# A fused LoRA kernel: how the first load of x is cut over partitions

## The chip, the cores and the metric

The kernel runs on one core of one Trainium2 chip. The metric is device time in microseconds for one execution; lower is better. The kernel before took 123.53 us (median of three runs, 123.52 to 123.67).

A core has TensorE (PE, matrix products), VectorE (DVE), ScalarE (ACT), GpSimd (POOL) and SyncE (SP), which here issues all transfers. Transfers between the chip's main memory and the on-chip memory (128 partitions, each a row of bytes) are carried out by 16 DMA engines. A transfer increments a semaphore by 16 when it is complete, and other engines wait for that count.

## The reference

```python
x: (16, 512, 768) float32    A: (768, 16)    B: (16, 768)    scale = 0.5

lora = np.matmul(np.matmul(x, A), B)
return (x + scale * lora).astype(np.float32)
```

x is 8192 tokens of 768 numbers, 25.2 MB; the result is as large. Every byte of x is read once and every byte of the result is written once.

## The kernel before

A tile is 128 tokens, one in each partition, 768 numbers (3 KB) each. The 64 tiles are cut into five parts of 8, 8, 16, 16 and 16 tiles (`PARTS`). Within a part, each partition holds consecutive tokens: a part of 8 tiles gives a partition one run of 8 x 3 KB = 24 KB of main memory, and a transfer of n tiles of it takes n x 3 KB from each partition's run. x stays in one buffer, `x_sb`, which has room for the first four parts; the fifth reuses the first's and second's room. The sum is written over x there and stored from there.

Loads are listed by part, first tile and number of tiles:

```python
LOADS = [
    (0, 0, 2), (0, 2, 6), (1, 0, 8), (2, 0, 8), (2, 8, 8), (3, 0, 16), (4, 0, 8), (4, 8, 8)
]
```

Load 0 brings two tiles (128 rows of 6 KB), load 1 the other six of part 0 (128 rows of 18 KB). Load k has a semaphore `s_load[k]` of its own.

SP issues in this order (`on_sync`, line 136): load 0, load 1 (line 139), after a wait the rows of A in three transfers (line 156; 12 rows of 4 KB to partitions 0 to 11), after another wait the rows of B (line 160; 16 rows of 3 KB to every fourth partition from 0), then loads 2 to 5. When the sums of the first two parts are done, and PE has reached a certain place in the third group, it issues stores 0 and 1 (line 149); when store 0 has landed, load 6 goes into its room, and load 7 when store 1 has. Stores 2 and 3 follow their sums, and store 4 is issued at the end (line 356).

Compute goes by groups of 8 tiles. `narrowed` (line 188) casts half a group from float32 to float16 (line 196): it waits for the loads that hold the tiles (line 193), once per engine and load. In the first group POOL casts tiles 0 and 1 (load 0), and ACT casts tiles 2 and 3 and then 4 to 7 (load 1). In later groups ACT casts the first four tiles and POOL the other four. DVE turns the result in blocks (line 255), PE multiplies with a spread-out A (line 285, `ps_yt`), ACT scales into `y_bd` (line 240), PE multiplies with B (line 306, `lora_ps`), and DVE adds that to x (line 260).

The weights are prepared at the beginning: DVE turns A's rows (line 248), after A's transfers and POOL's first cast; POOL then casts B (line 214), and makes `w_one` and `w_bd` (lines 216 and 222) from the turned A. PE needs `w_bd` and the turned x before its first product of line 285.

Every engine runs its own written order; semaphores connect them.

Of the kernel before, what the change touches and what calls it, by code (L numbers as in the profile page):

```python
# [28 lines left out]
def kernel(  # L29
# [10 lines left out]
    P = 128  # L40
# [3 lines left out]
    x2 = x.flatten_outer_dims()  # L44
# [38 lines left out]
    def sem(name):  # L83
        sems.append(nc.alloc_semaphore(name))
        return sems[-1]
# [10 lines left out]
    def memory(t2, i, s, n):  # L96
        S = PARTS[i]
        return t2[ds(parts[i], S * P), :].rearrange("(p s) d -> p s d", s=S)[:, ds(s, n), :]

    def held(i, s, n):  # L100
        return tiles(where.index((i, s)), n)

    def tiles(t, n):
        return x_all[:, ds(t % ROOM, n), :]

    LOADS = [
        (0, 0, 2), (0, 2, 6), (1, 0, 8), (2, 0, 8), (2, 8, 8), (3, 0, 16), (4, 0, 8), (4, 8, 8)
    ]
    s_load = [sem(f"s_load{k}") for k in range(len(LOADS))]

    def load_of(t):
        i, s = where[t]
        return next(k for k, ld in enumerate(LOADS) if ld[0] == i and ld[1] <= s < ld[1] + ld[2])
# [21 lines left out]

    def on_sync(e):
        def load(k):
            ld = LOADS[k]
            e.dma_start(out=held(*ld), in_=memory(x2, *ld)).then_inc(s_load[k], 16)  # L139

        def summed(k):
            e.wait_ge(s_sum, k + 1)
            if STORED[k] + 1 < NG:

                e.sem_inc(s_free[PAIRS - 1], 1)

        def store(k, done):
            st = STORES[k]
            e.dma_start(out=memory(out2, *st), in_=held(*st)).then_inc(done, 16)

        load(0)
        load(1)
        e.wait_ge(s_ready, 1)
        blocks = A.rearrange("(c e) r -> c (e r)", e=64)
        for c in range(SETS):
            e.dma_start(
                out=a_rows[c : SET * SET : SET, :], in_=blocks[ds(c * SET, SET), :]
            ).then_inc(s_a, 16)
        e.wait_ge(s_brows, 1)
        e.dma_start(out=b_rows[0 : R * APART : APART, :], in_=B).then_inc(s_b, 16)  # L160
        for k in range(2, len(LOADS) - 2):
            load(k)

        for p in range(2, PAIRS):
            e.sem_inc(s_free[p], 1)
        summed(0)
        summed(1)


        e.wait_ge(s_lora, 2 * PAIRS + 2)  # L170
        store(0, s_out0)
        store(1, s_out1)
        e.wait_ge(s_out0, 16)
        load(len(LOADS) - 2)
        e.wait_ge(s_out1, 16)
        load(len(LOADS) - 1)
        for k in range(2, len(STORES)):
            summed(k)
            if k == 2:


                e.wait_ge(s_raise, 6)
            if k + 1 < len(STORES):
                store(k, s_out)
# [3 lines left out]
    def narrowed(e, copy, g, first, n=SUB):  # L188
        t = g * GROUP + first
        for k in dict.fromkeys(load_of(t + k) for k in range(n)):  # L190
            if (e, k) not in here:
                here.add((e, k))
                e.wait_ge(s_load[k], 16)
        if g:
            e.wait_ge(s_taken, g)
        ins = copy(out=xn[:, ds(first, n), :], in_=tiles(t, n))  # L196

        ins.then_inc(s_narrow if g else s_first if first else s_a, 1)

    def on_gpsimd(e):  # L200
        e.memset(a_rows[0:Q], 0.0).then_inc(s_ready, 1)  # L201
        e.memset(b_rows, 0.0).then_inc(s_brows, 1)  # L202
        e.memset(pick, 0.0).then_inc(s_pick, 1)
        e.memset(w_bd.rearrange("p c k m -> p (c k m)").bitcast(fp32), 0.0)  # L204
        e.memset(y_bd.rearrange("p s m -> p (s m)").bitcast(fp32), 0.0).then_inc(s_ready, 1)  # L205
        e.wait_ge(s_pick, 1)
        e.affine_select(  # L207
            out=pick, in_=pick, compare_op=mybir.AluOpType.not_equal, fill=1.0, base=0,
            pattern=[[0, NQ], [-APART, Q]], channel_multiplier=1,
        ).then_inc(s_pick, 1)  # L210
        narrowed(e, e.tensor_copy, 0, 0, SUB // 2)
        e.wait_ge(s_pick, 2)
        e.wait_ge(s_b, 16)
        e.tensor_copy(out=b_half, in_=b_rows).then_inc(s_bh, 1)  # L214
        e.wait_ge(s_ready, 3)
        e.tensor_copy(  # L216
            out=w_one.rearrange("i (c e) k r -> i c e (k r)", c=SETS),
            in_=a_t[0:Q].rearrange("i k r (e c) -> i c e (k r)", c=SET)[:, 0:SETS, 0:SET, :],
        ).then_inc(s_w, 1)
        e.wait_ge(s_w, 1)  # L220
        for b in range(NQ):
            e.tensor_copy(  # L222
                out=w_bd[ds(b * Q, Q), :, :, ds(b * Q, R)], in_=w_one
            ).then_inc(s_w, 1)
            e.wait_ge(s_w, b + 2)
        for g in range(1, NG):
            narrowed(e, e.tensor_copy, g, SUB)

    def on_scalar(e):
        narrowed(e, e.copy, 0, SUB // 2, SUB // 2)  # L230
        narrowed(e, e.copy, 0, SUB)
        e.wait_ge(s_bp, 1)
        e.copy(out=b_mm, in_=lora[0][:, 0, :]).then_inc(s_bm, 1)  # L233
        for g in range(NG):
            if g + 1 < NG:
                narrowed(e, e.copy, g + 1, 0)
            e.wait_ge(s_y, g + 1)
            for b in range(NQ):
                q = ds(b * Q, Q)
                last = e.mul(out=y_bd[q, :, q], in_=y_ps[q, :, :], mul=sc)  # L240
                if b == 0 and g + 1 < NG:

                    last.then_inc(s_narrow, 1)
            last.then_inc(s_spread, 1)
# [151 lines left out]
```

## Time and profile before

| What | Value |
|---|---|
| median of three runs | 123.53 us |
| the profiled execution's own time | 123.47 us |
| its span | 121.7 us |
| DMA packets (rows and small completion writes) | 1928, 50.43 MB |
| DMA engines' packet time, share of 16 engines' span | 97.0% |
| DVE busy | 81.7 us (67%) |
| PE busy | 50.7 us (42%) |
| ACT busy | 37.4 us (31%) |
| POOL busy | 28.4 us (23%) |

The span is from the first to the last instruction on the core; the time has a small part around it. The page divides the span into 40 slices of 3.04 us: a digit is the busy share in tenths, and a row in GB/s says what the DMA engines moved. A table of stretches gives the same for stretches that one chooses. In a row of the timeline, the bracket says how long the engine had been idle and what released it.

### The profile page before, as it was taken

The page shows a single profiled execution, that of the slowest core. Times are in us where ns is not written, and L with a number is a line of the kernel's source. Part 1 is how long each engine was busy: PE and PEld are TensorE (multiplying, and loading weights), DVE is VectorE, ACT ScalarE, POOL GpSimd, SP SyncE. Part 2 cuts the span into 40 slices and gives each one's busy share as a digit, 9 for nine tenths or more (in the row PEclk, how much of TensorE's full clock was granted, in tenths as well). Part 3 has the DMA queues.
Part 4 walks back from the last instruction along what each step waited for, and adds up shares of the span by engine and source line. Part 5 has one row for each costly group of instructions (what it writes and reads, how often), then busy time and mean ns, then how long its engine had stood idle before and what let it go on. Part 6 is the DMA issues. An engine that isn't in the chain of part 4 may idle for free.

```text
span 121.7 us, 889 instructions
## 1 busy us (share of the span) xinstructions
PE 50.7 (42%) x322; PEld 29.6 (24%) x322; DVE 81.7 (67%) x42; ACT 37.4 (31%) x43; POOL 28.4 (23%) x24
## 2 busy tenths in 40 slices
PE   0000239477457647745745744774674320000000
PEld 0000026243323424423423322442442110000000
DVE  0002850599999999999999989999995991000000
ACT  4003928526409313644440192733004000000000
POOL 7721638017009002604400170710000000000000
PEclk9999999999999999999999999999999995555555
DMA  3999999999998997999999999997998899799790
GB/s 65 442 418 440 444 420 428 444 420 428 477 517 355 420 517 307 452 412 436 452 396 428 460 404 436 469 517 323 452 517 388 388 517 436 339 517 452 323 517 0
DMA packets 1928, 50.43 MB, mean 414 GB/s; under 512 B 236, under 2 KB 236, under 8 KB 392
## 3 DMA queue, kind: packets, MB, share of 16 engines
q1 hardware_dynamic: 1928, 50.43, 97.0%
HBM read 25.26 MB, written 25.17 MB: 414 GB/s over the span
## 4 chain that ended last, share of the span: by engine, by line
DVE 34%; DMA 28%; PE 10%; ACT 9%; issue 1%; SPq 0%; POOLq 0%
DVE x_sb L260 22%; DMA x_sb<-in_x_dram 20%; DVE xt L255 12%; DMA out_dram<-x_sb 8%; PE ps_yt L285 6%; ACT xn L196 6%; PE lora_ps L306 3%; ACT y_bd L240 3%; SPq L139 0%; SPq L391 0%; POOLq L134 0%; POOLq L377 0%
## 5 line engine op out<-in xcount | busy, mean ns | idle before, releaser
L260 DVE TENSOR_TENSOR x_sb<-x_sb,lora_ps 128x1536 f32<-128x1536 f32 x32 | 53.7, 1734 | 1.4 <-PE lora_ps L306 1.4
L306 PE MATMUL lora_ps<-b_mm,y_bd 128*128 128x512 f16 (+1 forms) x128 | 25.0, 328 | 22.4 <-ACT y_bd L240 14.1
L196 ACT CAST xn<-x_sb 128x3072 f16<-128x3072 f32 (+1 forms) x9 | 23.4, 2609 | 35.4 <-DMA x_sb<-in_x_dram 25.7
L285 PE MATMUL ps_yt<-xt,w_bd 128*128 128x256 f16 x192 | 26.1, 288 | 12.7 <-DVE xt L255 12.7
L255 DVE STREAM_TRANSPOSE xt<-xn 128x3072 f32<-128x3072 f32 (+1 forms) x9 | 27.0, 3005 | 6.5 <-ACT y_bd L240 6.1
L196 POOL CAST xn<-x_sb 128x3072 f16<-128x3072 f32 (+1 forms) x8 | 20.7, 2586 | 44.7 <-DMA x_sb<-in_x_dram 26.2
L285 PEld LDWEIGHTS ps_yt<-xt,w_bd 128*128 128x128 f16 x192 | 18.9, 101 | 20.6 <-issue 15.8
L306 PEld LDWEIGHTS lora_ps<-b_mm,y_bd 128*128 128x128 f16 x128 | 10.6, 98 | 35.3 <-ACT y_bd L240 16.4
L240 ACT ACTIVATE y_bd<-ps_yt 32x256 f16<-32x256 f32 x32 | 12.0, 374 | 19.5 <-PE ps_yt L285 19.1
L248 DVE STREAM_TRANSPOSE a_t<-a_rows 32x1024 f32<-32x1024 f32 x1 | 1.9, 1943 | 11.3 <-DMA a_rows<-in_A_dram 11.3
L319 PE MATMUL lora_ps<-b_half,pick 128*128 128x512 f16 (+1 forms) x2 | 0.8, 500 | 12.5 <-POOL b_half L214 12.5
L319 PEld LDWEIGHTS lora_ps<-b_half,pick 128*128 128x128 f16 x2 | 0.1, 106 | 12.5 <-issue 12.5
L222 POOL COPY w_bd<-w_one 32x384 f16<-32x384 f16 x4 | 2.0, 499 | 0.2
L214 POOL CAST b_half<-b_rows 128x768 f16<-128x768 f32 x1 | 0.8, 827 | 4.6 <-DMA b_rows<-in_B_dram 4.6
L196 ACT ACT_TABLE_LOAD x1 | 1.3, 1283 | 0.9 <-PEq L377 0.9
L204 POOL MEMSET w_bd<- 128x1536 f32 x1 | 1.4, 1372 | 0.0
L201 POOL MEMSET a_rows<- 32x1024 f32 x1 | 0.9, 941 | 0.5 <-POOLq L134 0.5
L216 POOL CAST w_one<-a_t 32x384 f16<-32x384 f32 x1 | 0.8, 849 | 0.9 <-DVE a_t L248 0.9
L233 ACT CAST b_mm<-lora_ps 128x768 f16<-128x768 f32 x1 | 0.8, 798 | 0.0
L202 POOL MEMSET b_rows<- 128x768 f32 x1 | 0.7, 727 | 0.0
L205 POOL MEMSET y_bd<- 128x512 f32 x1 | 0.5, 514 | 0.0
L207 POOL TENSOR_SCALAR_AFFINE_SELECT pick<-pick 128x128 f16<-128x128 f16 x1 | 0.3, 298 | 0.0
(5 smaller groups left out, 0.6 us busy)
## 6 DMA issues: line engine op xcount, KB each, us to landing
out_dram<-x_sb SPq DMA_DIRECT2D x3, 6144.0 KB, 19.4
x_sb<-in_x_dram SPq DMA_DIRECT2D x5, 3072.0 KB, 14.6
x_sb<-in_x_dram SPq DMA_DIRECT2D x1, 6144.0 KB, 41.6
out_dram<-x_sb SPq DMA_DIRECT2D x2, 3072.0 KB, 13.8
x_sb<-in_x_dram SPq DMA_DIRECT2D x1, 2304.0 KB, 9.7
x_sb<-in_x_dram SPq DMA_DIRECT2D x1, 768.0 KB, 4.6
a_rows<-in_A_dram SPq DMA_DIRECT2D x3, 16.0 KB
b_rows<-in_B_dram SPq DMA_DIRECT2D x1, 48.0 KB, 7.5
```

The lines of the kernel that those rows point to most:

```text
L196: ins = copy(out=xn[:, ds(first, n), :], in_=tiles(t, n))
L201: e.memset(a_rows[0:Q], 0.0).then_inc(s_ready, 1)
L204: e.memset(w_bd.rearrange("p c k m -> p (c k m)").bitcast(fp32), 0.0)
L214: e.tensor_copy(out=b_half, in_=b_rows).then_inc(s_bh, 1)
L222: e.tensor_copy(out=w_bd[ds(b * Q, Q), :, :, ds(b * Q, R)], in_=w_one).then_inc(s_w, 1)
L240: last = e.mul(out=y_bd[q, :, q], in_=y_ps[q, :, :], mul=sc)
L248: e.transpose(out=a_t[0:Q].rearrange("i k r c -> i (k r) c"), in_=a_rows[0:Q].rearrange("c (i k r) -> c (k r) i", k=2, r=R),).then_inc(s_r ...
L255: return e.transpose(out=ts[0], in_=ts[1])
L260: ins = e.tensor_tensor(out=xs, in0=xs, in1=lora[p % 2], op=mybir.AluOpType.add)
L285: mm = e.matmul(y_ps, w_bd[:, c, k, :], xv[:, :, c, :, k], start=(m == 0), stop=(m == MMS - 1),)
L306: mms.append(e.matmul(t[:, k, ds(n0, w)], y_bd[:, 2 * p + k, :], b_mm[:, ds(n0, w)], start=True, stop=True,))
L319: last = e.matmul(lora[0][:, 0, ds(n0, w)], pick.rearrange("p b r -> p (b r)"), b_half[:, ds(n0, w)], start=True, stop=True,)
```

## The change

Load 0 and load 1 still bring the first part's eight tiles, the same 128 x 24 KB. The cut between them is another. Load 0 is now two transfers: the first brings all eight tiles of partitions 0 to 15 (16 rows of 24 KB, `HEAD = 16`), the second brings tiles 0 and 1 of partitions 16 to 127 (112 rows of 6 KB). Load 1 brings tiles 2 to 7 of partitions 16 to 127 (112 rows of 18 KB). Both transfers of load 0 increment `s_load[0]`, so that whoever waits for load 0 waits for 32 instead of 16; the other loads keep 16. Which engine waits for which load stays the same: POOL's first cast for load 0, ACT's first two for load 1. All other loads, all stores and all compute stay as they were.

```diff
+    HEAD = 16
+    SHARES = {
+        0: [(slice(0, HEAD), slice(0, 8)), (slice(HEAD, P), slice(0, 2))],
+        1: [(slice(HEAD, P), slice(2, 8))],
+    }
+    needs = [16 * len(SHARES.get(k, [0])) for k in range(len(LOADS))]
...
         def load(k):
-            ld = LOADS[k]
-            e.dma_start(out=held(*ld), in_=memory(x2, *ld)).then_inc(s_load[k], 16)
+            i, s, n = LOADS[k]
+            for rows, cols in SHARES.get(k, [(slice(0, P), slice(s, s + n))]):
+                n = cols.stop - cols.start
+                e.dma_start(
+                    out=held(i, cols.start, n)[rows], in_=memory(x2, i, cols.start, n)[rows]
+                ).then_inc(s_load[k], 16)
...
-                e.wait_ge(s_load[k], 16)
+                e.wait_ge(s_load[k], needs[k])
```

## The prediction

> **What bounds the kernel now.** I read the page's slices first, then the DMA lines, then the table of stretches, then the chain of work that ended last. The page's own rows:
>
> ```profile
> span 121.7 us, 889 instructions
> ...
> DMA  3999999999998997999999999997998899799790
> GB/s 65 442 418 440 444 420 428 444 420 428 477 517 355 420 517 307 452 412 436 452 396 428 460 404 436 469 517 323 452 517 388 388 517 436 339 517 452 323 517 0
> DMA packets 1928, 50.43 MB, mean 414 GB/s; under 512 B 236, under 2 KB 236, under 8 KB 392
> ...
> q1 hardware_dynamic: 1928, 50.43, 97.0%
> ```
>
> The DMA digits are 9 nearly everywhere from the second slice to the last but one, and the queue's packets fill 97.0% of 16 engines' span. No compute engine comes near that. A few 7s and 8s could still be gaps, so I asked for stretches (us from the start, then each engine's busy time, the TensorE clock, the DMA share and the rate):
>
> ```profile
> 0.00:2.00 2.00, 0.00 (x0) 0.00 (x0) 0.00 (x0) 1.11 (x1) 1.23 (x6) 1.00 0.15 18
> 2.00:3.00 1.00, 0.00 (x0) 0.00 (x0) 0.00 (x0) 0.17 (x1) 1.00 (x3) 1.00 0.82 154
> 3.00:4.00 1.00, 0.00 (x0) 0.00 (x0) 0.00 (x0) 0.00 (x0) 1.00 (x1) 1.00 0.92 375
> 4.00:5.00 1.00, 0.00 (x0) 0.00 (x0) 0.00 (x0) 0.00 (x0) 0.82 (x3) 1.00 1.23 479
> 5.00:9.00 4.00, 0.00 (x0) 0.00 (x0) 0.00 (x0) 0.00 (x0) 1.46 (x1) 1.00 1.01 433
> ...
> 20.00:30.00 10.00, 6.61 (x40) 3.80 (x39) 7.25 (x4) 5.60 (x6) 4.18 (x2) 1.00 1.01 433
> 60.00:70.00 10.00, 6.04 (x43) 3.62 (x41) 10.00 (x6) 1.89 (x5) 0.36 (x1) 1.00 1.01 430
> 110.00:119.00 9.00, 0.00 (x0) 0.00 (x0) 0.00 (x0) 0.00 (x0) 0.00 (x0) 0.50 1.01 437
> ```
>
> Packets are counted where they start, so a short stretch can show more than 1.00. What counts is that loads (5 to 9), loads with the compute running (20 to 30), stores with loads (60 to 70) and stores alone (110 to 119) all run at 430 to 437 GB/s with a share of 1.01. I take 433 GB/s as the full rate. The transfers are the bound from about 2 us to the end, and nothing in them is idle that could take up a delay. The only stretch below the rate is the start: against 433, the third microsecond misses 0.279 MB and the fourth 0.058, while the fifth is 0.046 ahead, in all 0.291 MB or 0.67 us.
>
> The compute side follows the transfers, as the chain shows (start, length, what):
>
> ```profile
> 1.33 9.72 DMA x_sb<-in_x_dram
> ...
> 11.08 4.13 ACT xn L196 x2
> ...
> 15.24 1.79 DVE xt L255
> ...
> 17.16 5.16 PE ps_yt L285 x24
> ...
> 22.75 3.38 DVE xt L255
> ...
> 44.70 10.29 DMA out_dram<-x_sb
> ...
> 55.01 14.58 DMA x_sb<-in_x_dram
> ```
>
> Load 1 ends 1.33 + 9.72 = 11.05 us after the start, the casts on ACT begin at once, and from there to the first stores at 44.70 one thing releases the next. So a late load 1 makes those stores late by the same time, and a late store 0 makes the loads of the last part late (55.01). When the loads come late at the front, both the queue and the compute that feeds it are shifted together.
>
> **The change, part by part.** These rows are needed; first the instructions in order of time (start, length), then issues (KB each, us from issue to landing), then one line's issue times in ns (least, median, most):
>
> ```profile
> 0.89 0.86 SPq L139 DMA_DIRECT2D x_sb<-in_x_dram  x2
> ...
> 1.94 2.00 SPq L156 DMA_DIRECT2D a_rows<-in_A_dram  x3
> ...
> 4.57 2.04 SPq L139 DMA_DIRECT2D x_sb<-in_x_dram  x4
> 5.51 1.46 POOL L196 CAST xn<-x_sb 128x1536 f16<-128x1536 f32 x1 [0.65 <-DMA x_sb<-in_x_dram]
> 11.08 4.13 ACT L196 CAST xn<-x_sb 128x1536 f16<-128x1536 f32 x2 [8.91 <-DMA x_sb<-in_x_dram]
> 11.28 1.94 DVE L248 STREAM_TRANSPOSE a_t<-a_rows 32x1024 f32<-32x1024 f32 x1 [11.28 <-DMA a_rows<-in_A_dram]
> 11.57 0.83 POOL L214 CAST b_half<-b_rows 128x768 f16<-128x768 f32 x1 [4.60 <-DMA b_rows<-in_B_dram]
> ```
>
> ```profile
> L139 SPq DMA_DIRECT2D x_sb<-in_x_dram x8: 340/426/575, 0.9 to 62.5; - x8
> ```
>
> *One more issue on SP.* Load 0 becomes two instructions, load 1 stays one. At the median of 0.43 us, everything behind on SP is issued 0.43 us later: A's three transfers from 1.94, B's one, and loads 2 to 5 from 4.57. All of these stand in the rings behind load 1, which ends at 11.05, so about 6 us of queued rows cover the 0.43 us. Price 0; without the cover 0.43 us.
>
> *Load 0 grows.* It brought 128 rows of 6 KB (0.786 MB) and now brings 16 rows of 24 KB and 112 of 6 KB: 393 + 688 = 1.081 MB. At the full rate that lands (1.081 - 0.786)/433 = 0.68 us later. Only POOL waits for it (32 instead of 16 at L193, then the 1.46 us cast at 5.51). Queued behind on POOL is the cast of b_half, which waits until 11.57 for B, after 4.60 us of idle time, and then w_one and w_bd, for which PE waits; DVE's first transpose also waits for POOL's cast but got A's rows only at 11.28. So load 0 may land 4.60 us later before anyone notices, and B itself comes later when the rings do. Price 0; beyond the 4.60 us, one for one.
>
> *Load 1 shrinks* from 128 to 112 rows of 18 KB. The sum of loads 0 and 1 is 3.146 MB before and after, 7.27 us at the full rate, and each of 16 engines still has 1 row of 24 KB and 7 each of 6 and 18, that is 192 KB as before. With every engine at its full rate, load 1 ends where it did.
>
> *What is new is the shape.* In every bulk transfer of the trace, 16 engines write into all 128 partitions at once. Now the first one has 16 engines writing into 16 neighbouring partitions, and the next two have them in 112. No transfer of x shows what few partitions take in, so I bound it. From below: they take whatever comes, 393 KB in 0.91 us, price 0. From above: a partition takes no more than its 128th of 433 GB/s, which is 3.38 GB/s; then a 24 KB row lasts 7.27 us instead of 0.91, price +6.4 us. The nearest row in the trace is the stretch in which A and B were loaded, 9.9 to 10.67 us:
>
> ```profile
> DMA packets 83, 0.44 MB, mean 567 GB/s; under 512 B 41, under 2 KB 41, under 8 KB 69
> ```
>
> The 28 packets between 2 and 8 KB are A's 12 rows of 4 KB and B's 16 of 3 KB (the page's 392 - 236 = 156 are these and load 0's 128). A's 12 rows go to partitions 0 to 11: 49 KB in at most 0.77 us, 64 GB/s or 5.3 GB/s a partition. So partitions can take more than 3.38 GB/s, and 6.4 us is too much. At 5.3 GB/s a partition, 16 partitions take 85 GB/s, the first transfer lasts 393/85 = 4.6 us instead of 0.91, and the price is **+3.7 us**. I take it as the nearest row, knowing that those 12 rows may have asked for no more than they got; that is why zero stays as the lower end.
>
> *The 112 rows.* From below 0 (each engine moves seven rows at its full rate). If the partitions are what limits, 112 of them at their ordinary share need as long as 128 did, 7.27 us for 6 + 18 KB instead of 6.36: **+0.9 us**. From above, if engines meet in pairs at the same partitions all the way, 6.36 us once more. I take 0.9, since no row shows pairs meeting.
>
> *The start-up.* The 0.67 us lost before 5 us is a wait for first rows. It could shrink with one long row for each engine, so from 0 to -0.67; I take 0, as a narrow first transfer would hide it.
>
> *What a delay meets.* Load 1, A and B, then the compute shift by 4.6 us, and the first stores with them. The end is the last store:
>
> ```profile
> 101.51 0.33 SPq L356 DMA_DIRECT2D out_dram<-x_sb  x1
> ```
>
> ```profile
> DMA to landing us min/median/max: 19.4/19.4/19.4
> ```
>
> It lands at 101.51 + 19.4 = 120.9 us, while its 6144 KB need 6.29 MB / 433 = 14.5 us: it stands behind other stores for some 4.9 us. The compute could thus be 4 us quicker at its end and nothing would change; the queue sets the end, and it holds the delay entirely. Sum: 3.7 + 0.9 = +4.6 us. The profiled execution took 123.47 us (span 121.7 and 1.77 around it), 0.06 under the median of 123.53, so 123.47 + 4.6 = **128.1 us**.
>
> [...]
>
> **The rivals.**
>
> *Nothing is narrow, and the start improves.* The mechanism is the first wait: 128 short rows are opened from 2 to 4 us at 154 and 375 GB/s; with 16 long ones each engine opens one row and then streams 0.91 us. Ceiling 0.67 us, 122.8; perhaps half, 123.1. For it: the loss is there, and A's and B's small rows went by without a visible dip. Against: a first row must be opened in any case. It decides only if 16 engines into 16 partitions lose less than 0.67 us.
>
> *Nothing is narrow, nothing is gained.* The start costs the same and the extra issue is hidden: 123.5 us. For it: same bytes per engine, same queue.
>
> *Narrow, but partly passed by.* Some of the 16 engines get their row through early and go on to the other 112 partitions while the rest wait; the engines end unequally and the lag is some 1 to 2.5 us: about 125 us. Against: an engine's rows go in order, and all 16 begin with a row for these partitions.
>
> *Narrow everywhere.* Pairs of engines meet in the 112 rows as well: 3.7 + 6.4 = +10.1 us, 133.6 us. Against: 128 rows run at 433 GB/s, so the split over engines seems to keep them apart; but 7 rows an engine instead of 8 shifts that split.
>
> **How the numbers follow.** Forecast 0.55 (its own range reaches from 126.2 to 131: A's rows need not have filled their window of 0.77 us, and if they took 0.6 the 16 partitions take 109 GB/s, the first term is 2.7, and with no cost for the 112 rows the time is 126.2; at the other end about half of the 6.4 us of pairs meeting comes on top of 3.7); passed by 0.13; narrow everywhere 0.10; better start 0.13; no change 0.09. The range from 123.3 to 131.0 leaves out the case narrow everywhere and most of the better start, about 0.19. About 0.2% (0.25 us) is what a measurement of this kernel can tell from no change. Faster 0.13, same 0.09, slower 0.55 + 0.13 + 0.10 = 0.78.
>
> **What would show it.** In the changed kernel's stretches, 2 to 6 us should run at about 85 GB/s in place of 154 to 479, with the DMA share still near 1 (the rows last, the engines do not idle). POOL's cast should move from 5.51 to about 9.9 (0.68 + 3.7 later), ACT's from 11.08 to about 15.7, DVE's first transpose with it, and the stores of 44.70 to about 49.3; from there on every stretch at 433 again. If ACT's cast starts within 0.5 us of 11.08, the narrow entrance does not exist and the whole sum falls. If POOL's moves as said but ACT's moves by much more than 4.6, the 112 rows cost more than 0.9. The prediction would be wrong on the path if ACT's cast is late but the last store is not: then there was slack in the queue that the share of 1.01 did not show.

## The result and the profile after

The changed kernel takes 128.75 us (median of 4 runs, 128.63 to 128.95) against 123.58 us before on the same chip. The ratio is 1.0419, with a 95% interval from 1.0401 to 1.0437. That is 5.17 us slower; the prediction was 128.1 us and slower.

The page of the changed kernel, its slices and DMA lines:

```profile
span 127.0 us, 890 instructions
...
DMA  8699999999999899899999999999699979997990
GB/s 124 110 298 343 271 449 418 441 426 433 426 503 464 372 403 495 356 426 441 426 364 441 418 449 403 488 480 464 294 495 480 449 310 495 480 449 310 495 480 16
DMA packets 1928, 50.43 MB, mean 397 GB/s; under 512 B 252, under 2 KB 252, under 8 KB 392
...
q1 hardware_dynamic: 1928, 50.43, 97.3%
```

The bytes are the same, and the DMA engines are as busy as before (97.3% of the span). Only the GB/s row tells the difference: the second to fifth slices show 110, 298, 343 and 271, where before they showed 442, 418, 440 and 444. From the sixth slice on the rate is the old one. A DMA engine that looks busy is therefore not always one at its rate: from 8 to 16 us the share is 0.99 at 283 GB/s, from 20 to 30 us 1.00 at 430.

The same in stretches (us, busy time of the engines, clock, DMA share, GB/s):

```profile
2.00:6.00 4.00, 0.00 (x0) 0.00 (x0) 0.00 (x0) 0.17 (x1) 2.82 (x5) 1.00 0.75 111
6.00:8.00 2.00, 0.00 (x0) 0.00 (x0) 0.00 (x0) 0.00 (x0) 0.00 (x0) 1.00 1.18 381
8.00:16.00 8.00, 0.00 (x0) 0.00 (x0) 0.00 (x0) 0.00 (x0) 1.46 (x1) 1.00 0.99 283
20.00:30.00 10.00, 6.22 (x31) 4.12 (x32) 4.07 (x2) 5.24 (x7) 3.97 (x4) 1.00 1.00 430
```

There are two slow stretches: 2 to 6 us at 111 GB/s and 8 to 16 us at 283 GB/s. A row counts whole where it starts, so these are means over mixed rows: seven of the 16 rows of 24 KB start before 2 us, and rows of 6 KB from 4.3 us on; from 8 us come most of the 112 rows of 18 KB. Stretches cut at the rows' starts separate them. From 1.9 to 4.3 us only the 16 rows of 24 KB start, and from 7.4 to 14.2 us only the 112 rows of 18 KB, with 16 completion writes (packets, MB, share of 16 engines):

```profile
q1 hardware_dynamic: 16, 0.39, 106.9%
```

```profile
q1 hardware_dynamic: 128, 2.06, 107.4%
```

Share times length times 16, divided by the rows, is the mean time of one: 1.069 x 2.4 us = 2.57 us for a row of 24 KB, which lasts 0.92 us at the full rate (20 to 30 us before: 4.33 MB, 176 rows, share 1.01), and 1.04 us for one of 18 KB, which lasted 0.69 us before (5 to 9 us). What this does to the engines is in the timeline (the casts' line 196 is 208 here, the loads' line 139 is 149):

```profile
0.89 1.32 SPq L149 DMA_DIRECT2D x_sb<-in_x_dram  x3
...
8.34 1.46 POOL L208 CAST xn<-x_sb 128x1536 f16<-128x1536 f32 x1 [3.48 <-DMA x_sb<-in_x_dram]
16.06 4.12 ACT L208 CAST xn<-x_sb 128x1536 f16<-128x1536 f32 x2 [13.89 <-DMA x_sb<-in_x_dram]
16.26 1.93 DVE L260 STREAM_TRANSPOSE a_t<-a_rows 32x1024 f32<-32x1024 f32 x1 [16.26 <-DMA a_rows<-in_A_dram]
16.55 0.83 POOL L226 CAST b_half<-b_rows 128x768 f16<-128x768 f32 x1 [6.74 <-DMA b_rows<-in_B_dram]
```

POOL's first cast moved from 5.51 to 8.34 (+2.83) and ACT's from 11.08 to 16.06 (+4.98). The issue of the first transfer (KB, us from issue to landing):

```profile
x_sb<-in_x_dram SPq DMA_DIRECT2D x1, 384.0 KB, 5.4
```

The 384 KB of the first transfer take 5.4 us to land, where before twice as many bytes in 128 rows took 4.6. From ACT on the chain is the old one, later: the first stores are issued at 49.67 in place of 44.70 (+4.97).

### The profile page after: what moved, and what is told of

The parts are those of the page before. It is cut to its first block, busy times and chain, and to the rows that moved or that the text cites. A ratio compares the mean times of both kernels' runs of the same rounds, so it can differ in the third digit from the quotient of the medians.

```text
span 127.0 us, 890 instructions
## 1 busy us (share of the span) xinstructions
PE 50.7 (40%) x322; PEld 29.7 (23%) x322; DVE 81.7 (64%) x42; ACT 37.5 (30%) x43; POOL 28.4 (22%) x24
## 3 DMA queue, kind: packets, MB, share of 16 engines
q1 hardware_dynamic: 1928, 50.43, 97.3%
## 4 chain that ended last, share of the span: by engine, by line
DVE 33%; DMA 31%; PE 9%; ACT 8%; issue 1%; SPq 1%; POOLq 0%
DMA x_sb<-in_x_dram 23%; DVE x_sb L272 21%; DVE xt L267 12%; DMA out_dram<-x_sb 8%; PE ps_yt L297 6%; ACT xn L208 5%; PE lora_ps L318 3%; ACT y_bd L252 3%; SPq L149 1%; SPq L403 0%; POOLq L142 0%; POOLq L389 0%
## 6 DMA issues: line engine op xcount, KB each, us to landing
x_sb<-in_x_dram SPq DMA_DIRECT2D x1, 2016.0 KB, 14.2
```

## The experiments

Three questions: is it the 16 partitions, the memory that is read, or the cut into 112 rows; what decides which partitions crowd; and does the start gain anything from long rows. Most kernels add one transfer to the kernel before and change nothing else, so that its time against before is the price of that transfer. The added one goes to the room of part 3, which load 5 overwrites; SP issues load 5 after it has landed:

```diff
+        e.dma_start(
+            out=held(3, 0, 8)[DESTINATION], in_=memory(x2, 0, 0, 8)[SOURCE]
+        ).then_inc(s_extra, 16)
         load(0)
         load(1)
...
         for k in range(2, len(LOADS) - 2):
+            if k == 5:
+                e.wait_ge(s_extra, 16)
             load(k)
```

**Sixteen rows, near and far.** e1_near has DESTINATION `0:16` and SOURCE `0:16`; e2_far `0:128:8` and `0:16`; e3_rows `0:16` and `0:128:8`.

> The kernel before, with one transfer more at the very front: 16 rows of 24 KB (part 0's first 16 runs, read a second time) into partitions 0 to 15 of the room that load 5 fills later. 0.393 MB more, 0.91 us at 433 GB/s. Theory N (what counts is how close together the partitions are that the 16 engines write at the same time): the transfer lands about 5.4 us after its issue, as it did in the changed kernel, and the time rises by 0.91 plus 1.7 to 2.7, to 126.2 to 127.2 us. Theory M (the memory side is slow, because 16 engines read one contiguous 393 KB): the same here. Theory S (nothing is slow but the cut of loads 0 and 1 into 112 rows): lands after about 3.7 us, time 124.5 us.

> As e1_near, but the same 16 rows of memory go to partitions 0, 8, 16 to 120. Theory N: fewer engines meet, so landing after 3.7 to 4.6 us and a time of 124.5 to 125.4 us. Theory M: as in e1_near, because the memory read is the same. Theory S: 124.5 us.

> As e1_near, into partitions 0 to 15, but read from every eighth run of part 0 in place of the first 16 (the values there are not used). Theory N: as e1_near, 126.2 to 127.2 us and a landing of 5.4 us. Theory M: faster than e1_near by the 1.7 to 2.7 us. Theory S: 124.5 us.

Against a before of 123.33 us: e1_near 126.34 us (+3.01; ratio 1.0254, 1.0236 to 1.0273), e2_far 125.21 (+1.88; 1.0139 to 1.0173), e3_rows 126.55 (+3.22; 1.0251 to 1.0291). The added transfer's line in e1_near, then in e2_far, then in e3_rows:

```profile
x_sb<-in_x_dram SPq DMA_DIRECT2D x1, 384.0 KB, 5.4
```

```profile
x_sb<-in_x_dram SPq DMA_DIRECT2D x1, 384.0 KB, 4.1
```

```profile
x_sb<-in_x_dram SPq DMA_DIRECT2D x1, 384.0 KB, 5.9
```

In e1_near the 384 KB land after 5.4 us, the figure of the changed kernel. The same rows of memory into spread partitions land after 4.1 us; other rows of memory into the near partitions do not get faster (5.9). So it is the destination, not the memory. Of e1_near's 3.01 us, 0.91 are the bytes. The crowding is at least the 1.13 us by which it exceeds e2_far, and at most the other 2.10: the far one too costs twice its bytes. Its issue takes SP 0.60 us in place of 0.39, which may be a part of that, and e5_128 below also pays 0.75 us beyond its bytes.

**The 112 rows alone.** e4_112 adds 112 rows of 24 KB to partitions 16 to 127; e5_128 adds the same bytes as 128 rows of 21 KB.

```diff
-            out=held(3, 0, 8)[16:128], in_=memory(x2, 0, 0, 8)[16:128]
+            out=held(3, 0, 7)[0:128], in_=memory(x2, 0, 0, 7)[0:128]
```

> The kernel before, with one transfer more at the front: 112 rows of 24 KB into partitions 16 to 127 of the room that load 5 fills later, 2.75 MB, 6.36 us at 433 GB/s. If 112 rows, 7 an engine, run at the full rate: 129.9 us. If a partition takes its ordinary share and no more (the prediction's 0.9 us for 24 KB): 130.8 us. If the engines meet at the partitions, as load 1 of the changed kernel suggests (16.03 - 8.25 = 7.8 us for 2.06 MB, 1.6 times the full rate's 4.77): 133 to 134 us.

> The control for e4_112: the kernel before, with one transfer more at the front that brings the same 2.75 MB, but as 128 rows of 21 KB. If the bytes alone cost e4_112 its time, this takes the same 133.7 us. If it is the cut into 112 rows of 7 an engine, this runs at the full rate: 6.36 us more than before, 129.7 to 129.9 us.

e4_112 took 133.69 us (+10.36 on 123.33), e5_128 130.47 us (+7.11 on 123.36). Equal bytes, 3.2 us apart. The added transfer of each:

```profile
x_sb<-in_x_dram SPq DMA_DIRECT2D x1, 2688.0 KB, 13.5
```

```profile
x_sb<-in_x_dram SPq DMA_DIRECT2D x1, 2688.0 KB, 9.1
```

The expected 133 to 134 us came out: the cut into 112 rows in partitions 16 to 127 cost these 3.2 us by itself. The prediction's 0.9 us for it was too little by more than 2. The control took some 0.7 us more than its 6.36 us of bytes.

**One size changed.** e7_head64 is the changed kernel with 64 rows in place of 16 at the head.

```diff
-    HEAD = 16
+    HEAD = 64
```

> The changed kernel with one size changed, HEAD 64 for 16: 64 rows of 24 KB, then 64 rows of 6 KB and 64 of 18 KB; every engine has 4 rows of each, the same 192 KB. [...]

131.42 us (1.0651, 1.0632 to 1.0670): 8.06 us over before. Four rows of each size on an engine cost more than the changed kernel's one and seven (5.17 us).

**Strides.** e8_stride2 has DESTINATION `0:32:2`, e9_stride7 `0:112:7`, both SOURCE `0:16`.

> As e1_near and e2_far (one transfer of 16 rows of 24 KB more at the front), into partitions 0, 2, 4 to 30. [...] Theory D (what counts is the distance of the partitions): closer to e1_near's 126.3 us than to e2_far's, because the 16 rows lie within 31 partitions and e2_far's within 121.

> The same into partitions 0, 7, 14 to 105. [...] Theory D: as e2_far, 125.2 us. If a transfer of 16 rows always costs twice its bytes: 125.2 us too.

e8_stride2 125.38 us (+2.02; 1.0145 to 1.0182), e9_stride7 125.00 us (+1.64; 1.0116 to 1.0159). The 16 rows within 31 partitions cost what the 16 within 121 cost (2.02 and 1.88 us): distance is not it, theory D falls. e9_stride7's interval overlaps e2_far's (1.0139 to 1.0173), so by itself it separates nothing.

**The same number of neighbours, elsewhere.** e11_low64 has DESTINATION `0:64`, e12_mid64 `32:96`, both SOURCE `0:64`. This is the pair that decides.

> The kernel before, with one transfer more at the front: 64 rows of 24 KB into partitions 0 to 63. 1.57 MB, 3.63 us at the full rate, 4 rows an engine. [...] If 64 partitions of 128 simply take half the rate: 7.3 us.

> The same 64 rows of memory into partitions 32 to 95: also 64 neighbouring partitions, also 4 rows an engine. [...] If 64 partitions of 128 take half the rate wherever they lie: as e11_low64, 130.3 to 131 us.

e11_low64 took 131.71 us (+8.26 on 123.45; 1.0651 to 1.0682), e12_mid64 128.03 us (+4.58; 1.0335 to 1.0382). They differ by 3.68 us, and 1.57 MB at 433 GB/s are 3.63. Both are about 1 us above the time of their bytes, 7.26 us at half the rate and 3.63 at the full one; e5_128 was 0.75 above. While the added rows come, the stretch of e11_low64 is:

```profile
2.00:9.00 7.00, 0.00 (x0) 0.00 (x0) 0.00 (x0) 0.17 (x1) 2.82 (x5) 1.00 1.06 225
```

and e12_mid64's:

```profile
2.00:6.00 4.00, 0.00 (x0) 0.00 (x0) 0.00 (x0) 0.17 (x1) 2.82 (x5) 1.00 0.97 338
6.00:9.00 3.00, 0.00 (x0) 0.00 (x0) 0.00 (x0) 0.00 (x0) 0.00 (x0) 1.00 1.05 416
```

From 2 to 9 us all 64 rows of e11_low64 start and nothing else: 225 GB/s, half the full rate, with the DMA share at 1.06, so that a row of 24 KB lasts 1.86 us, twice its 0.92. Partitions 32 to 95, as many, take 338 GB/s in a stretch that holds the start-up. So 64 partitions did not take half the rate wherever they lay: 0 to 63 did (+8.26 us), 32 to 95 did not (+4.58).

**Another order.** e6_behind is the changed kernel with the 16 rows behind the 112.

```diff
-        0: [(slice(0, HEAD), slice(0, 8)), (slice(HEAD, P), slice(0, 2))],
-        1: [(slice(HEAD, P), slice(2, 8))],
+        0: [(slice(HEAD, P), slice(0, 2))],
+        1: [(slice(HEAD, P), slice(2, 8)), (slice(0, HEAD), slice(0, 8))],
...
-        for k in dict.fromkeys(load_of(t + k) for k in range(n)):
+        for k in dict.fromkeys([load_of(t + k) for k in range(n)] + ([1] if t + n <= 8 else [])):
```

> The changed kernel's three transfers in another order: 112 rows of 6 KB, 112 of 18 KB, then the 16 rows of 24 KB; POOL's first cast and ACT's wait for all three. Theory E: the crowding belongs to the shapes, in any order, so part 0 lands about 5 us late again, and the time is 128 to 129.5 us. Theory C (it is the cold start: 16 engines begin at once and stay in step): the 16 rows come at a time when the engines have drifted apart, and the time falls by 1 us or more, to 127.5 us or less.

131.06 us (1.0609, 1.0565 to 1.0654; 130.01 to 131.71): slower than the change, which neither theory gave. Theory C falls: by the trace's packet records (start and length of each row) the 16 rows start 1.2 us apart here (0.3 in the changed kernel) and still last 2.75 us each. ACT's cast and DVE's first transpose in e6_behind:

```profile
17.96 4.13 ACT L208 CAST xn<-x_sb 128x1536 f16<-128x1536 f32 x2 [15.79 <-DMA x_sb<-in_x_dram]
...
19.56 1.94 DVE L260 STREAM_TRANSPOSE a_t<-a_rows 32x1024 f32<-32x1024 f32 x1 [19.56 <-POOL xn L208]
```

Part 0 is there 1.9 us later than in the changed kernel (17.96 against 16.06), and DVE's transpose now waits for POOL's cast, which came last (19.56 against 16.26). Summed over the rows of part 0, an engine's packets take 13.3 us here and 12.8 in the changed kernel, which is 0.5 of the 1.9 us. The rest is not explained; that in the changed kernel part of the crowding passes in the start-up, which would be lost anyway, is a guess.

**The start.** e10_whole loads part 0 as one transfer of 128 rows of 24 KB.

```diff
-        (0, 0, 2), (0, 2, 6), (1, 0, 8), (2, 0, 8), (2, 8, 8), (3, 0, 16), (4, 0, 8), (4, 8, 8)
+        (0, 0, 8), (1, 0, 8), (2, 0, 8), (2, 8, 8), (3, 0, 16), (4, 0, 8), (4, 8, 8)
...
         load(0)
-        load(1)
...
-        for k in range(2, len(LOADS) - 2):
+        for k in range(1, len(LOADS) - 2):
```

> The kernel before with part 0 in one load: 128 rows of 24 KB, no load 1. This tries the prediction's rival on the start by itself: every engine opens one 24 KB row first, and 128 partitions are written, so no engine meets another. If the start-up loss of 0.67 us shrinks with long rows: faster by 0.2 to 0.6 us, 122.8 to 123.2 us. If a first row has to be opened in any case: within 0.25 us of before (POOL's first cast then starts at about 11 in place of 5.5, which the wait for B until 11.57 hides but for 1 us, and the stores have room for that). If long first rows cost more, as e5_128 hints with 0.7 us more than its bytes: 123.8 to 124.1 us.

123.97 us against 123.45 (1.0053, 1.0036 to 1.0069; single times from 123.48 to 124.53). The gain of 0.2 to 0.6 us that long rows might have brought did not come; the median lies among the 123.8 to 124.1 us of the case in which long first rows cost more. ACT's first cast, which waits for all of part 0:

```profile
11.17 4.12 ACT L195 CAST xn<-x_sb 128x1536 f16<-128x1536 f32 x2 [8.99 <-DMA x_sb<-in_x_dram]
```

It starts 0.09 us later than the 11.08 with short rows first, so part 0 is there no sooner: long first rows gained nothing at the start. Why the median lies 0.5 us higher can't be read from this trace, which is of the fastest execution; it stays open. The kernel also moves POOL's first cast from 5.51 to 11.20 us, and with it DVE's first transpose from 11.28 to 12.69, so that the 0.5 us need not be the rows'.

## Why the prediction was right, point by point

**The bound and the path: right.** The prediction held that nothing in the transfers is idle, so that a delay at the front reaches the end whole. ACT's cast is 4.98 us later, the first stores 4.97, the span 5.3. The remaining 0.3 us arose later: load 6, issued 4.98 us later, landed after 15.26 us in place of 14.58 in the chain of waits (the stretch from 60 to 70 us ran at 406 GB/s in place of 430), and the last store, landing after 19.0 us in place of 19.4, gave 0.4 of that back. The trace does not show why.

**The extra issue and the late load 0: right.** SP's three transfers of A are issued from 2.26 in place of 1.94, and nothing waited for that. POOL's cast came 2.83 us later, where 4.4 were expected, and POOL then still idled 6.74 us for B.

**The first transfer: right in kind, too dear.** It was priced at +3.7 us, from A's twelve rows at 64 GB/s, 85 GB/s for 16 partitions. e1_near puts it between 1.13 and 2.10 us. The packet records of the changed kernel allow an estimate of 1.5: the 16 rows last 2.57 us, against 1.74 for the first sixteen rows of 24 KB in e10_whole, which also open the queue, and the first sixteen rows of 6 KB behind them 0.90 us in place of 0.23 (0.83 + 0.67). The 64 GB/s were a lower end: the prediction said that A's rows may have asked for no more than they got, and the trace of the kernel before shows it, since each of A's packets lasts 0.16 us, 26 GB/s for its engine, near a sixteenth of 433. (A's rows go to partitions 0, 4, 8 and 12, then 1, 5, 9 and 13, then 2, 6, 10 and 14, four in each transfer, not to 0 to 11; the 5.3 GB/s a partition is the same.) Of the signs, 2 to 6 us ran at 111 GB/s where 85 were expected and at a share of 0.75 where nearly 1 was: rows that start before 2 us are counted there, and cut at 1.9 and 4.3 us the share is 1.07.

**The 112 rows: too cheap, and the step that failed.** "I take 0.9, since no row shows pairs meeting" was too low a choice between 0 and 6.4. e4_112 against e5_128 gives 3.2 us. In the changed kernel itself: POOL's delay of 2.83 is 0.68 for more bytes and 2.15 of crowding (the 16 rows and the 112 of 6 KB); ACT's delay is 2.15 more although load 1 has 0.68 us fewer bytes, so 2.83 of crowding in the 112 rows of 18 KB. Together 4.98. The packets agree: 1.04 us in place of 0.69 for each of an engine's seven rows of 18 KB is 2.5 us. The sum of 4.6 came near by luck, because one term was too high and the other too low, not because both were known.

**The mechanism.** In these runs the time depended on which partitions were written together (e1_near +3.01 us, e2_far +1.88), not on the memory read (e3_rows +3.22), not on their distance (e8_stride2 +2.02), not on their number (e11_low64 +8.26, e12_mid64 +4.58).

The rows behind the added transfer tell it without the start-up: in these kernels they are 128 rows of 6 KB, 0.23 us each at the full rate (their median in the kernel before). By the packet records the first sixteen of them last 0.84 us (median) behind partitions 0 to 15 (e1_near, the longest 0.90), 0.46 behind e2_far, 0.47 behind e8_stride2, 0.48 behind 0 to 63 (e11_low64), and 0.23 behind 32 to 95 (e12_mid64) and behind all 128 (e5_128). That is up to four times, twice and once. Behind e9_stride7 they last 0.45, about as behind e2_far. What lies behind these ratios no run shows. In the changed kernel the 393 KB for partitions 0 to 15 took from 1.9 us to their landing at 6.3, about 90 GB/s with the start-up.

**Why 112 rows crowd** is only argued. Of 112 partitions, 64 lie in the upper half (64 to 127) and 48 in the lower; if the upper half takes half the rate and no more (the lower took 225 of 433 GB/s in e11_low64, and e7_head64, which loads one half behind the other, shows 219, 170, 246 and 199 GB/s in its second to fifth slices), it alone needs as long as it did with 128 rows, which is the 0.9 us, an estimate. The rest of e4_112's 3.2 us is not explained; which partitions an engine takes in such a transfer no trace here shows.

**The rivals.** Nothing narrow with a better start is refuted by e1_near and e10_whole; nothing narrow without one by e1_near. "Partly passed by" did not happen: the 16 rows end within 0.7 us of each other (4.31 to 4.98), and the engines start their rows of 18 KB within 0.2 us (7.42 to 7.63). "Narrow everywhere" is what the kernel does in kind; its price of 6.4 us for the 112 rows was about twice what e4_112 shows.

## What to carry to other kernels

A transfer that had a row for every DMA engine and the same bytes on each still ran at half the rate (225 of 433 GB/s into partitions 0 to 63) or less (a row of 24 KB lasted 2.57 us in place of 0.92 into 0 to 15), because it was the partitions written at one time that counted: cut loads along the free dimension, with all 128 partitions in each piece, as the kernel before did (123.58 against 128.75 us), or at least try partitions as in 32 to 95 (+4.58 us) rather than 0 to 63 (+8.26). When such a cut is priced, price each of its pieces: the remainder of 112 rows cost more (3.2 us in e4_112) than the head of 16 (at most 2.10 in e1_near). And read the GB/s row beside the DMA digits, since the engines looked as busy at 283 GB/s (share 0.99) as at 430 (1.00).

## What the runs showed of the hardware that was not expected

- 64 partitions took 225 GB/s at 0 to 63, while at 32 to 95 the same transfer cost 3.68 us less.
- 112 rows of 24 KB, an equal number for each of 16 engines, cost 3.2 us more than the same bytes in 128 rows.
- The issue on SP of 16 rows with a stride of 8 partitions took 0.60 us, against 0.39 us for 16 neighbours.
- Rows behind a crowded transfer paid too, though they went to all 128 partitions: 6 KB rows lasted up to 0.90 us behind 0 to 15, 0.23 behind 32 to 95.
- Long first rows did not shorten the start: part 0 reached ACT at 11.17 us with 24 KB rows, at 11.08 with 6 KB rows first.
